# Seven stretches of an attention stage get written orders of TensorE, VectorE and ScalarE, and the softmax's join stands in one piece

## The chip, the cores and the metric

The kernel runs on one core of one Trainium2 chip. Its engines work side by side, each through a queue of its own in order: TensorE (PE, with its weight loads shown as PEld), VectorE (DVE), ScalarE (ACT), GpSimd (POOL) and SyncE (SP, which issues nearly all transfers). The metric is the device time of one execution in microseconds; the kernel before took 1698.79 us (median of three runs, 1698.14 to 1699.94).

## The reference

A decoder trunk of two layers over 512 tokens of width 1024: attention and a gated convolutional FFN, then a Mamba-2 mixer and a second FFN, all in float32. The change lies in the attention, cut here to what matters:

```python
def dilated_attention_mixer(h, w_qkv, w_o, cos, sin):
    qkv = (h @ w_qkv).reshape(bsz, s, N_ATTN_GROUPS, 3, HEADS, HEAD_DIM)   # 3 groups, 8 heads of 128
    q = apply_partial_rope(qkv[:, :, :, 0], cos, sin)                      # first 32 of 128 rotated
    k = apply_partial_rope(qkv[:, :, :, 1], cos, sin)
    for g in range(N_ATTN_GROUPS):                                         # dilations 1, 4, 16
        o_g, lse_g = dilated_window_attention(q[:, :, g], k[:, :, g], v[:, :, g], dil, steps)
    wts = jax.nn.softmax(jnp.stack(lses, axis=2), axis=2)
    o = jnp.einsum("bsgh,bsghe->bshe", wts, jnp.stack(outs, axis=2))
    return o.reshape(bsz, s, OUT_WIDTH) @ w_o
```

## The kernel before

The input stands transposed, in eight tiles of 128 features by 512 tokens, each as a high and a low part (`xh`, `xl`). Every product with weights is done in three passes: high x high, high x low, low x high. So each unit of weights (512 KB) comes by a transfer into one of four `raw` buffers, ScalarE casts its high part, and VectorE subtracts to get the low part (`load_unit`, L128). A unit is 24 products of TensorE over 512 tokens.

The opening computes the values of groups 1 and 2 for heads 0 to 3 (`first`, `second`, from `v_steps`), the sums of squares for the norm (`ssum`, then `ss` on TensorE, `ms` on VectorE, `rcol` on GpSimd), and `combine`: 32 small pieces on VectorE that form sums and differences of input tiles. These serve the pairs: for the query and key of one group, `qk_pair` uses seven half-width products in place of eight, from four weight pieces `a` to `d` (`load_sevens`: sums at L317 to L321, lows at L331).

Then one head after the other. `attend(h)` is a generator: the scores of four blocks of 128 queries (`scores`), maxima and exponentials, `join`, `by_key`, `values`. A row's two softmax parts (group 0; groups 1 and 2) lie on different partitions, so `join` copies 16 small pieces (`oth`, L591), then takes eight steps on 128x8 elements with one exponential between (L594 to L602). Its result, the share, multiplies the probabilities (`pr`, L609), which TensorE transposes (`pp`, L612) to multiply them with the values. Between these pieces TensorE computes the query, key and value of head h + 1 (`qk_step`, `qk_pair`, `v0_step`); VectorE reads each product, shuffles 32 rows (`rotqk`), and GpSimd turns them with two instructions of its own (L464 and L465, or L474 and L475).

What sets the order: TensorE's instructions stand as written wherever `tc.manual_schedule` names PE. VectorE's and ScalarE's are placed by the framework's scheduler, which sets each instruction of those engines where it reckons its operands ready.

Of the kernel before, what the change touches and what calls it, by code (L numbers as in the profile page):

```python
# [53 lines left out]
def trunk(ctx: ExitStack, tc: tile.TileContext, A, out):  # L54
# [12 lines left out]
    s3 = att.__enter__()  # L67
# [363 lines left out]
    dma(mask, A["mask"])  # L431
    V.tensor_tensor(cr, cr, rbc, op=ALU.mult)
    V.tensor_tensor(sr[0:ROPE, :], sr[0:ROPE, :], rbc[0:ROPE, :], op=ALU.mult)
# [20 lines left out]

    def qk_step(h, g, c, cut=None):
        n = f"qk{h}{g}{c}"
        p = project(A["wqk"][h * 7 + 2 * g + c], n, cut=cut)
        t = t2(n, "qk", 10, s3)
        at, of = (in_blocks, by_residue) if g == 0 else ((lambda ap: ap),) * 2
        V.tensor_tensor(at(t), of(p), of(cr), op=ALU.mult)  # L460
        rot = t2("rot" + n, "rot", 2, s3)
        R = slice(0, ROPE)
        V.stream_shuffle(rot[R, :], p[R, :], SWAP)  # L463
        G.tensor_tensor(rot[R, :], rot[R, :], sr[R, :], op=ALU.mult)  # L464
        G.tensor_tensor(at(t)[R], at(t)[R], of(rot)[R], op=ALU.add)  # L465
        qk[h, g, c] = t

    def turn(t, n):

        rot = t2("rot" + n, "rot", 2, s3)  # L470
        R = slice(0, ROPE)
        V.stream_shuffle(rot[R, :], t[R, :], SWAP)
        V.tensor_tensor(t, t, cr, op=ALU.mult)
        G.tensor_tensor(rot[R, :], rot[R, :], sr[R, :], op=ALU.mult)  # L474
        G.tensor_tensor(t[R, :], t[R, :], rot[R, :], op=ALU.add)  # L475

    def qk_pair(h, g):

        n = f"qk{h}{g}"
        sums, split_weights = load_sevens(  # L480
            A["wqs"][QK_PAIRS.index((h, g))], n, lambda n: t2(n, "sq", 2)
        )
        sums()
        w = {}
        r1, r3, r2 = (mm_bank(f"{n}r{i}")[:, 0:256] for i in (1, 3, 2))
        r4 = aux_bank(f"{n}r4")[:, 0:256]
        kept = t2("kept" + n, "ssum", 2)
        s1, s5 = kept[:, H0], kept[:, H1]
        q, k = (t2(f"{n}{c}", "qk", 10, s3) for c in range(2))

        def products(dst, t, at, operand, begin):
            if t not in w:
                w[t] = split_weights(t)
            for j in range(KD // 2):
                mm3(dst, *w[t], at + j, *operand(j), begin and j == 0, j == KD // 2 - 1, skip=True)

        def plain(b, h):
            return lambda j: (xh[2 * j + b][:, h], xl[2 * j + b][:, h])

        def other(i, h):  # L500
            return lambda j: [t[:, h] for t in combined[j][i]]

        products(r1, "a", 0, plain(0, H0), True)
        SC.copy(s1, r1)
        products(r3, "a", 4, other(0, H0), True)
        SC.copy(s5, r3)
        products(r2, "b", 0, other(0, H1), True)
        V.tensor_tensor(q[:, H1], s1, r2, op=ALU.add)
        products(r4, "b", 4, other(1, H1), True)
        products(r1, "c", 0, plain(1, H0), False)  # L510
        SC.copy(q[:, H0], r1)
        products(r3, "c", 4, plain(1, H1), False)
        V.tensor_tensor(q[:, H1], q[:, H1], r3, op=ALU.add)
        turn(q, n + "0")
        products(r2, "d", 0, other(1, H0), False)
        V.tensor_tensor(k[:, H0], s1, r2, op=ALU.add)
        V.tensor_tensor(k[:, H1], k[:, H0], s5, op=ALU.add)
        V.tensor_tensor(k[:, H0], k[:, H0], r4, op=ALU.add)
        turn(k, n + "1")
        qk[h, g, 0], qk[h, g, 1] = q, k  # L520

# [15 lines left out]
    def qk_steps(h):  # L537
        steps = []
        for g in range(NG):
            if (h, g) in QK_PAIRS:  # L540
                steps += [lambda g=g: qk_pair(h, g), lambda: None]
            else:
                steps += [lambda cut=None, g=g, c=c: qk_step(h, g, c, cut) for c in range(2)]
        return steps + [lambda: v0_step(h)]

# [3 lines left out]
    def attend(h):  # L549
# [35 lines left out]

        def join():

            V.tensor_copy(own[:, 2], own[:, 0])
            for a in range(4):
                for b in range(4):  # L590
                    V.tensor_copy(oth[32 * b : 32 * b + 32, :, :, a], own[32 * a : 32 * a + 32, 1:3, :, b])  # L591
            w = sm.tile([P, 5, 2, 4], F32, tag="join", name="join", bufs=2)
            top, ex, f = w[:, 0], w[:, 1:3], w[:, 3]
# [10 lines left out]

        def by_key(i):
            k0 = P if i == 0 else 0
            pr = prs[i]
            for w, cs in enumerate((slice(k0, 256), slice(256, 512))):
                V.tensor_scalar(pr[:, cs], pr[:, cs], share[:, w, i : i + 1], None, op0=ALU.mult)  # L609
            pp = (side_bank if i == 3 else aux_bank)("pp")  # L610
            for b in range(k0 // P, 4):
# [20 lines left out]
        scores(2)  # L632
        yield
        share = join()
        yield
        by_key(0)
        by_key(1)
        yield
        po, pg = aux_bank(f"po{h}"), aux_bank(f"pg{h}")
# [55 lines left out]

    with tc.manual_schedule(engines={mybir.EngineType.PE}):
        for f in qk_steps(0):
            f()

    def attend_and_project(h):  # L700

        core, fill = attend(h), qk_steps(h + 1)
        with tc.manual_schedule(engines={mybir.EngineType.PE}):
            next(core)
            v0_turn(h)
            fill[0]()
            fill[1]()
            next(core)
            next(core)
            for f in fill[2:5]:  # L710
                f()
            fill[5](cut=(2, lambda: next(core)))
            next(core)
            fill[6]()
            next(core, None)

    for h in range(NH):
        if h < NH - 2:
            attend_and_project(h)
            if h == STORED - 1:  # L720
                fetch_heads()
            if h == 3:
                for f in v_steps(1, 1)[1] + v_steps(2, 1)[1]:
                    f()
            continue
# [896 lines left out]
```

## Time and profile before

| what | us |
|---|---|
| median of three runs | 1698.79 |
| the profiled execution | 1699.21 |
| its span, first to last instruction | 1697.4 |
| the six heads 0 to 5, from the first product of head 0's stretch to that of head 6 | 382.76 |
| TensorE busy in the whole span | 1625.3 |
| VectorE busy in the whole span | 1235.5 |

A row of waits names the waiting engine, tile and line, then who released it, then the total in us, how many times, and the longest. A row of a stretch gives start and end, its length, the busy time of PE, PEld, DVE, ACT and POOL with the number of instructions, the clock granted to TensorE as a share of full speed, the share of the transfer engines, and GB/s. A row of a group gives line, engine, operation, output and inputs, count, busy us and mean ns of one, and the idle time ahead of it.

### The profile page before, as it was taken

To read this page: it belongs to the slowest core of one execution; us is meant where nothing else is said; L and a number is where in the kernel's file an instruction comes from. 1 tells how busy PE (TensorE), PEld (TensorE's weight loads), DVE (VectorE), ACT (ScalarE), POOL (GpSimd) and SP (SyncE) were. 2 spreads that over 40 slices of the span, in tenths; PEclk is the share of its full clock that TensorE was granted. 3 is DMA by queue.
4 is the path that set the end of the run, shared out by engine and by line. 5 is a ranking of instruction groups with operands and counts; after the bars stand their busy time and mean duration, and the time that the engine had idled before them with its cause. 6 is when DMAs were issued, how large, how long until landed. Compare 5 with 4: busy or idle time off the path is not lost.

```text
span 1697.4 us, 23559 instructions
## 1 busy us (share of the span) xinstructions
PE 1625.3 (96%) x8902; PEld 1416.5 (83%) x8902; DVE 1235.5 (73%) x2094; ACT 727.5 (43%) x1137; POOL 578.7 (34%) x432
## 2 busy tenths in 40 slices
PE   8987798997989999999999999999999999999998
PEld 6876687786878888998998888888888888988987
DVE  8566765637666677886875789989789777876874
ACT  6322232332423454444444545544444445344343
POOL 0253433304234245455333123212222356365230
PEclk8998898998989999999999999999999999999999
DMA  6222121321322332342332343332233232342241
GB/s 225 79 81 75 63 69 63 106 81 56 99 89 75 124 112 70 99 143 75 100 119 96 114 143 119 112 122 96 88 109 134 75 106 69 100 143 69 88 136 51
DMA packets 61889, 168.45 MB, mean 99 GB/s; under 512 B 7184, under 2 KB 10640, under 8 KB 61776
## 3 DMA queue, kind: packets, MB, share of 16 engines
q1 hardware_dynamic: 61216, 166.42, 29.5%
q8 instruction: 70, 1.15, 0.3%
q10 hardware_dynamic: 560, 0.53, 0.1%
q14 instruction: 43, 0.35, 0.1%
HBM read 163.19 MB, written 3.74 MB: 98 GB/s over the span
## 4 chain that ended last, share of the span: by engine, by line
PE 87%; DVE 9%; issue 2%; DMA 1%; ACT 1%; POOL 0%; SPq 0%; DVEq 0%; POOLq 0%; ACTq 0%
PE u L136 28%; PE qk L136 8%; PE v L136 6%; PE xs L136 5%; PE wso L136 5%; PE z L136 5%; PE b L136 3%; PE c L136 3%; PE wo L136 3%; PE wd L136 2%; PE wz L136 2%; DVE pr L609 1%; PE pp L612 1%; PE py L1195 1%; DVE oth L591 1%
## 5 line engine op out<-in xcount | busy, mean ns | idle before, releaser
L136 PE MATMUL u<-xh,hi_u 128*128 128x512 f32 x704 | 270.2, 384 | 0.0
L136 PE MATMUL u<-xh,lo_u 128*128 128x512 f32 x704 | 269.6, 383 | 0.0
L136 PE MATMUL u<-xl,hi_u 128*128 128x512 f32 x704 | 267.7, 380 | 0.0
L136 PEld LDWEIGHTS u<-xh,lo_u 128*128 128x128 f32 x704 | 131.9, 187 | 24.6
L128 DVE TENSOR_TENSOR lo_u<-raw_u,hi_u 128x1024 fp32r<-128x1024 f32 x88 | 124.3, 1422 | 38.6 <-ACT hi_u L127 38.5
L136 PEld LDWEIGHTS u<-xl,hi_u 128*128 128x128 f32 x704 | 132.0, 187 | 24.1
L136 PEld LDWEIGHTS u<-xh,hi_u 128*128 128x128 f32 x704 | 131.9, 187 | 22.5 <-issue 0.4
L127 ACT CAST hi_u<-raw_u 128x1024 fp32r<-128x1024 f32 x88 | 91.7, 1046 | 107.0 <-PE u L136 62.5
L464 POOL TENSOR_TENSOR rotqk<-rotqk,sr 32x512 f32<-32x512 f32 x32 | 54.2, 1694 | 224.5 <-DVE rotqk L463 214.1
L764 DVE SCALAR_TENSOR_TENSOR au<-u,par,au 128x511 f32<-128x511 f32 (+1 forms) x152 | 113.4, 746 | 20.4 <-ACT au L762 18.0
L789 POOL TENSOR_TENSOR au<-au,au 128x512 f32<-128x512 f32 x43 | 58.1, 1350 | 170.7 <-DVE au L764 156.9
L136 PE MATMUL qk<-xh,hi_qk 128*128 128x512 f32 x256 | 105.0, 410 | 0.1
L136 PE MATMUL qk<-xh,lo_qk 128*128 128x512 f32 x256 | 102.0, 398 | 0.0
L136 PE MATMUL qk<-xl,hi_qk 128*128 128x512 f32 x256 | 101.8, 398 | 0.0
L777 DVE TENSOR_TENSOR u<-u,rbc 128x512 f32<-128x512 f32 x76 | 52.9, 696 | 65.9 <-PE u L136 65.6
L1140 POOL TENSOR_TENSOR xdd<-xdt,dec 128x384 f32<-128x384 f32 x16 | 18.0, 1139 | 241.0 <-DVE xdt L1139 241.0
L460 DVE TENSOR_TENSOR qk<-qk,cr 128x512 f32<-128x512 f32 x32 | 22.0, 687 | 83.3 <-PE qk L136 83.2
L612 PE MATMUL pp<-ident,pr 128*128 128x128 f32 x120 | 24.0, 334 | 50.3 <-DVE pr L609 50.3
L762 ACT ACTIVATE au<-u,par 128x512 f32<-128x512 f32 x76 | 59.1, 778 | 23.0 <-DVE u L777 21.4
L612 PEld LDWEIGHTS pp<-ident,pr 128*128 128x128 f32 x120 | 16.0, 165 | 57.5 <-DVE pr L609 55.8
L239 POOL TENSOR_TENSOR ssum<-ssum,sq 128x512 f32<-128x512 f32 x21 | 32.5, 1549 | 84.4 <-ACT sq L238 84.0
L940 POOL TENSOR_TENSOR xr<-xr,sums 128x512 f32<-128x512 f32 x16 | 33.1, 2068 | 82.1 <-DVE sums L938 82.1
(3428 smaller groups left out, 4957.8 us busy)
## 6 DMA issues: line engine op xcount, KB each, us to landing
raw_u<-in_wup SPq DMA_DIRECT2D x88, 512.0 KB, 3.3
raw_qk<-in_wqk SPq DMA_DIRECT2D x32, 512.0 KB, 3.2
raw_xs<-in_win SPq DMA_DIRECT2D x16, 512.0 KB, 3.3
raw_z<-in_win SPq DMA_DIRECT2D x16, 512.0 KB, 3.3
lm<-rows SPq DMA_DIRECT2D x32, 256.0 KB, 5.0
raw_wso<-in_wso SPq DMA_DIRECT2D x16, 512.0 KB, 3.3
raw_v<-in_wv SPq DMA_DIRECT2D x12, 512.0 KB, 3.3
raw_wd<-in_wdn SPq DMA_DIRECT2D x16, 384.0 KB, 3.1
```

The source lines that it names most:

```text
L127: SC.copy(hi[:, s], raw[:, s])
L128: low.tensor_tensor(lo[:, s], raw[:, s], hi.bitcast(F32)[:, s], op=ALU.subtract)
L136: T.matmul(in_turns(dst), w, in_turns(x), start=first, stop=last, skip_group_check=skip)
L239: add.tensor_tensor(ssum, ssum, sq, op=ALU.add)
L460: V.tensor_tensor(at(t), of(p), of(cr), op=ALU.mult)
L464: G.tensor_tensor(rot[R, :], rot[R, :], sr[R, :], op=ALU.mult)
L612: T.transpose(pp[:, b * P : (b + 1) * P], pr[:, b * P : (b + 1) * P], ident)
L762: latest["tap"] = SC.activation(dst, src, AF.Identity, bias=col(c_b), scale=col(c_w + taps - 1))
L764: V.scalar_tensor_tensor(dst[:, j:], src[:, : S - j], col(c_w + taps - 1 - j), dst[:, j:], op0=ALU.mult, op1=ALU.add,)
L777: V.tensor_tensor(dst, p, rbc, op=ALU.mult)
L789: by.tensor_tensor(ab[1], ab[0], ab[1], op=ALU.mult)
L940: G.tensor_tensor(low3, low3, v.unsqueeze(1).to_broadcast([P, 2, 256]), op=ALU.add)
```

## The change

Seven stretches (from the second value product to the end of head 0's queries and keys, and the stretch of each of the heads 0 to 5) now stand in `manual_schedule` blocks for PE, DVE and Activation, so that these three engines take their instructions as written. For that, `qk_step` is cut into product and read, the loads into steps of their own (`ready`), `qk_pair` into the class `Pair` (sums, splits, seven blocks, the query's and the key's sums, swap and turn), and `by_key` loses the multiplication (`weigh`) and `join` the copies (`spread`). In a head, TensorE's first transposes move nine products later. In the first head's part, the plain product of the key moves behind both pairs. `combine` runs in the written stretch. The late values of head 3 are loaded two units ahead. One warm-up product (two instructions) is gone. Heads 6 and 7 keep the old order by `together`.

```diff
+            combine(0)
...
-    for j in range(KD // 2):
-        combine(j)
-    with tc.manual_schedule(engines={mybir.EngineType.PE}):
-        for f in second:
-            f()
-        T.matmul(warm[:, 0:P], ones, ones, start=True, stop=True)
...
+    def ready(h, g, c):
+        u = A["wqk"][h * 7 + 2 * g + c]
+        loaded[name_of(h, g, c)] = load_unit(u, name_of(h, g, c))
...
+    class Pair:
...
+        def key(self):
+            k = self.out[1]
+            V.tensor_tensor(k[:, H0], self.s[0], self.r[2], op=ALU.add)
+            V.tensor_tensor(k[:, H1], k[:, H0], self.s[1], op=ALU.add)
+            V.tensor_tensor(k[:, H0], k[:, H0], self.r[3], op=ALU.add)
+            self.swap(1)
+            self.turn(1)
+
+        def swap(self, c):
+            R = slice(0, ROPE)
+            rot = self.rot[c] = t2(f"rot{self.n}{c}", "rot", 2, s3)
+            V.stream_shuffle(rot[R, :], self.out[c][R, :], SWAP)
+            G.tensor_tensor(rot[R, :], rot[R, :], sr[R, :], op=ALU.mult)
+
+        def turn(self, c):
+            R = slice(0, ROPE)
+            t = self.out[c]
+            V.tensor_tensor(t, t, cr, op=ALU.mult)
+            G.tensor_tensor(t[R, :], t[R, :], self.rot[c][R, :], op=ALU.add)
+            qk[self.h, self.g, c] = t
...
+    WRITTEN = {E.PE, E.DVE, E.Activation}
+
+    with tc.manual_schedule(engines=WRITTEN):
+        load2(1)
+        V.tensor_tensor(cr, cr, rbc, op=ALU.mult)
+        second[0]()
+        combine(1)
+        load2(2)
...
+        second[3]()
+        one.sums()
+        one.split("ab")
+        p = qk_products(0, 0, 0)
+        qk_read(0, 0, 0, p)
+        one.split("cd")
...
+        two.key()
+        ready_v0(0)
+        p = qk_products(0, 0, 1)
+        qk_read(0, 0, 1, p)
+        ready(1, 0, 0)
+        v0_step(0)
+        ready(1, 0, 1)
...
     def attend_and_project(h, after=()):
+        core, m = attend(h), h + 1
+        follow = lambda c: ready(m + 1, 0, c)
+        with tc.manual_schedule(engines=WRITTEN):
+            pair = Pair(m, 1)
             next(core)
+            pair.sums((0,))
             v0_turn(h)
+            pair.split("a")
+            pair.sums((1,))
+            p = qk_products(m, 0, 0)
+            qk_read(m, 0, 0, p)
+            pair.split("bc")
+            ready(m, 2, 0)
+            p = qk_products(m, 0, 1)
+            qk_read(m, 0, 1, p)
+            next(core)
+            for i in range(3):
+                pair.block(i)
+            pair.query(0)
+            pair.split("d")
+            ready(m, 2, 1)
+            for i in range(3, 5):
+                pair.block(i)
+            next(core)
+            pair.block(5)
+            pair.query(1)
             next(core)
             next(core)
+            pair.block(6)
+            pair.turn(0)
+            pair.key()
+            ready_v0(m)
+            p = qk_products(m, 2, 0)
+            qk_read(m, 2, 0, p)
+
+            def cut():
+                next(core)
+                next(core)
+
+            p = qk_products(m, 2, 1, cut=(5, cut))
+            next(core)
+            qk_read(m, 2, 1, p)
+            for f in after[:2] or (lambda: follow(0), lambda: follow(1)):
+                f()
+            v0_step(m)
             next(core, None)
```

In the generator, each `next(core)` now runs to the next of nine stops: scores of blocks 0 and 1; of 2 and 3; `spread`; `join`; `weigh(0)` and `weigh(1)`; `by_key(0)` and `by_key(1)`; `weigh(2)` and `weigh(3)`; `values(0)`, `by_key(2)`, `by_key(3)`, `values(1)`; the rest.

Three places where the instructions move. First VectorE in head 1, around the join (`oth` and `join` its tiles, `qk21` head 2's pair, `lo_` and `raw` weights); before:

```order
L591 COPY oth<-own 32x4 x16
L128 TENSOR_TENSOR lo_qk_1734<-raw_qk_1732,hi_qk_1733 128x1024
L594 TENSOR_TENSOR join<-own,oth 128x8
L128 TENSOR_TENSOR lo_v_1815<-raw_v_1813,hi_v_1814 128x1024
L595 TENSOR_TENSOR join<-own,join 128x8
L596 TENSOR_TENSOR join<-oth,join 128x8
...
L600 TENSOR_TENSOR join<-join 128x8
L517 TENSOR_TENSOR qk_1576<-qk_1576,keptqk_1574 128x256
L318 TENSOR_TENSOR rawb_qk_2013<-rawa_qk_2012 128x512
L321 TENSOR_TENSOR q_qk_2015<-rawa_qk_2012,q_qk_2015 128x512
L601 RECIPROCAL join<-join 128x8
```

and now:

```order
L670 COPY oth<-own 32x4 x16
L527 TENSOR_TENSOR qk_1562<-qk_1562,qk21r_1558 128x256
L541 STREAM_SHUFFLE rotqk_1668<-qk_1562 32x512
L676 TENSOR_TENSOR join<-own,oth 128x8
L677 TENSOR_TENSOR join<-own,join 128x8
L678 TENSOR_TENSOR join<-oth,join 128x8
L680 TENSOR_TENSOR join<-own,join 128x8
L681 TENSOR_TENSOR join<-oth,join 128x8
L682 TENSOR_TENSOR join<-join 128x8
L683 RECIPROCAL join<-join 128x8
L684 TENSOR_TENSOR join<-join 128x8
L691 TENSOR_SCALAR pr<-pr,join 128x128
```

The eight steps of the join follow each other; the work for later weights has left this place. Second, the same engine and head a little later, at the other four multiplications; only now:

```order
L691 TENSOR_SCALAR pr<-pr,join 128x256 x3
L547 TENSOR_TENSOR qk_1562<-qk_1562,cr 128x512
L532 TENSOR_TENSOR qk_1563<-keptqk_1561,qk21r_1559 128x256
L533 TENSOR_TENSOR qk_1563<-qk_1563,keptqk_1561 128x256
L534 TENSOR_TENSOR qk_1563<-qk_1563,qk21r_1560 128x256
L541 STREAM_SHUFFLE rotqk_1702<-qk_1563 32x512
L547 TENSOR_TENSOR qk_1563<-qk_1563,cr 128x512
L128 TENSOR_TENSOR lo_v_1709<-raw_v_1707,hi_v_1708 128x1024
L465 TENSOR_TENSOR qk_1738<-qk_1713,cr 128x512
L468 STREAM_SHUFFLE rotqk_1740<-qk_1713 32x512
L691 TENSOR_SCALAR pr<-pr,join 128x256 x4
```

Before, all eight multiplications followed each other in one run (L609, x8 in the profile); now four stand ahead of the query's and key's turns and four behind, and the latter also behind the read of a product. Third, VectorE in the opening, between two sums of squares (`ssum`); before:

```order
L239 TENSOR_TENSOR ssum<-ssum,sq 128x512
L407 SCALAR_TENSOR_TENSOR ta3l<-d_419,par,ta3h 128x256
L415 TENSOR_TENSOR tb1l<-d_381,tb1h 128x256
L412 SCALAR_TENSOR_TENSOR d_400<-xp_218,par,t_401 128x256
L415 TENSOR_TENSOR tb3l<-t_420,tb3h 128x256
L415 TENSOR_TENSOR ta3l<-t_420,ta3h 128x256
L239 TENSOR_TENSOR ssum<-ssum,sq 128x512
```

and now:

```order
L239 TENSOR_TENSOR ssum<-ssum,sq 128x512
L228 SCALAR_TENSOR_TENSOR xl_98<-xp_259,par,xh_89 128x512
L128 TENSOR_TENSOR lo_v_252<-raw_v_250,hi_v_251 128x512
L239 TENSOR_TENSOR ssum<-ssum,sq 128x512 x2
L265 TENSOR_SCALAR ms<-ss 128x4
L128 TENSOR_TENSOR lo_v_316<-raw_v_314,hi_v_315 128x1024
L404 TENSOR_TENSOR d_325<-xp_119 128x256
```

The pieces of `combine` (L404 to L415) have left the opening and stand behind `ms`.

More of the change, by code (lines that the diff above doesn't have):

```diff
@@ L466, in qk_step @@
         qk[h, g, c] = t
[L468 to L493, printed above, removed]
-            for j in range(KD // 2):
[L495 to L520, printed above, removed]
@@ L537, in qk_steps @@
     def qk_steps(h):
[L538 to L544, printed above, removed]
+        return [
+            lambda cut=None, g=g, c=c: qk_step(h, g, c, cut) for g in range(NG) for c in range(2)
+        ] + [lambda: v0_step(h)]
+    E = mybir.EngineType
+    WRITTEN = {E.PE, E.DVE, E.Activation}
[5 more added lines that the diff above has]
+        load2(2)
+        V.tensor_tensor(sr[0:ROPE, :], sr[0:ROPE, :], rbc[0:ROPE, :], op=ALU.mult)
+        second[1]()
+        combine(2)
+        load2(3)
+        second[2]()
+        combine(3)
+        ready(0, 0, 0)
+        one = Pair(0, 1)
+        second[3]()
[4 more added lines that the diff above has]
+        one.split("cd")
+        two = Pair(0, 2)
+        for i in range(3):
+            one.block(i)
+        one.query(0)
+        two.sums()
+        two.split("a")
+        for i in range(3, 6):
+            one.block(i)
+        one.query(1)
+        two.split("b")
+        one.block(6)
+        one.turn(0)
+        one.key()
+        two.split("cd")
+        for i in range(3):
+            two.block(i)
+        two.query(0)
+        ready(0, 0, 1)
+        for i in range(3, 6):
+            two.block(i)
+        two.query(1)
+        two.block(6)
+        two.turn(0)
+        two.key()
[5 more added lines that the diff above has]
+        ready(1, 0, 1)
     scale = HD ** -0.5
@@ L584, in scores, with spread @@
                     )
-        def join():
+        def spread():
             V.tensor_copy(own[:, 2], own[:, 0])
@@ L694, in wo_first, with together, attend_and_project @@
         wo_held[m] = (hi, lo, p)
[L696 to L703, printed above, removed]
+    def together(core):
+        for n in (1, 1, 2, 2, 2, 1):
+            for _ in range(n):
+                next(core, None)
+            yield
+    def attend_and_project(h, after=()):
+        core, m = attend(h), h + 1
+        follow = lambda c: ready(m + 1, 0, c)
+        with tc.manual_schedule(engines=WRITTEN):
+            pair = Pair(m, 1)
@@ L715, in attend_and_project @@
+            qk_read(m, 2, 0, p)
[6 more added lines that the diff above has]
+            for f in after[:2] or (lambda: follow(0), lambda: follow(1)):
+                f()
+            v0_step(m)
             next(core, None)
+            for f in after[2:]:
+                f()
+            if after:
+                follow(0)
+                follow(1)
@@ L717, in trunk, with late_values @@
+    def late_values():
+        (l1, s1), (l2, s2) = v_steps(1, 1), v_steps(2, 1)
+        loads = [lambda l=l, u=u: l(u) for l in (l1, l2) for u in range(4)]
+        steps = s1 + s2
+        out = loads[:2]
+        for i, f in enumerate(steps):
+            if i + 2 < len(loads):
+                out.append(loads[i + 2])
+            out.append(f)
+        return out
     for h in range(NH):
         if h < NH - 2:
-            attend_and_project(h)
+            attend_and_project(h, late_values() if h == 3 else ())
```

85 lines of the change are left out of this document (69 added, 16 removed).

## The prediction

> **What bounds the kernel now.** I read the page first: which engine is nearly always busy, and where it is not.
>
> ```profile
> PE 1625.3 (96%) x8902; PEld 1416.5 (83%) x8902; DVE 1235.5 (73%) x2094; ACT 727.5 (43%) x1137; POOL 578.7 (34%) x432
> PE   8987798997989999999999999999999999999998
> PEclk8998898998989999999999999999999999999999
> ```
>
> TensorE (PE) is the bound, and what it lacks, some 72 of 1697.4 us, lies in the first 13 slices (42 us each), the attention; there its clock dips too. So a gain must come from PE's waits there. Next, PE's waits up to 600 us:
>
> ```profile
> PE pp L612 <- DVE pr L609: 50.3, 18, 7.8
> PE sc L571 <- POOL qk L475: 7.2, 1, 7.2
> PE v L136 <- DVE lo_v L128: 2.9, 2, 2.0
> PE ss L260 <- DVE ssum L239: 2.6, 1, 2.6
> ```
>
> 50.3 us is one wait, repeated: the transposes of the probabilities (`pp`) wait until VectorE has multiplied them by the softmax's share. The other rows are single waits before the first head. Third, one stretch per head, from its first projection product to the next head's (columns: length, then busy time of PE, PEld, DVE, ACT, POOL, granted clock, DMA share):
>
> ```profile
> 109.06:166.90 57.84, 48.70 (x279) 42.74 (x278) 35.55 (x82) 16.68 (x31) 22.30 (x12) 0.91 0.18 57
> 166.90:224.78 57.88, 48.73 (x278) 42.80 (x278) 37.13 (x92) 17.67 (x35) 22.28 (x12) 0.88 0.20 69
> 224.78:282.70 57.92, 48.77 (x279) 42.85 (x278) 37.15 (x92) 17.66 (x35) 22.28 (x12) 0.88 0.21 69
> 282.70:377.15 94.45, 90.88 (x470) 78.54 (x470) 47.45 (x104) 31.43 (x51) 21.17 (x12) 0.96 0.26 88
> 377.15:434.16 57.01, 47.84 (x279) 42.12 (x278) 36.85 (x88) 17.66 (x35) 22.32 (x12) 0.91 0.19 62
> 434.16:491.82 57.66, 48.21 (x278) 42.34 (x278) 37.84 (x93) 20.47 (x40) 18.37 (x12) 0.91 0.27 93
> ```
>
> Five heads lose about 9.1 us each; head 3, which also computes late values, loses 3.57 (94.45 - 90.88). Head 1 cut in four shows the price:
>
> ```profile
> 166.90:195.60 28.70, 28.70 (x174) 25.69 (x173) 19.70 (x62) 11.63 (x28) 9.37 (x6) 1.00 0.24 79
> 195.60:206.75 11.15, 2.00 (x8) 1.24 (x8) 11.15 (x22) 1.22 (x2) 8.22 (x4) 0.60 0.27 94
> 206.75:211.17 4.42, 4.42 (x13) 3.46 (x12) 1.09 (x3) 0.58 (x1) 1.26 (x1) 0.50 0.00 0
> 211.17:224.78 13.61, 13.61 (x88) 12.42 (x87) 5.19 (x7) 4.25 (x5) 3.42 (x2) 0.99 0.15 49
> ```
>
> PE waits 9.15 us (11.15 - 2.00) while VectorE is busy throughout; then it works 4.42 us at clock 0.50, 2.21 too many; the seven transposes in the hole, also at the low clock, lose some 1.0. So a head without the hole takes 57.88 - 9.15 - 2.21 - 1.0 = **45.5 us**. VectorE's 37.13 us would fit, 8 to spare: it is late by its order, not by its amount.
>
> **The heads.** The products stay. VectorE's order is now written: the spreading copies, the eight small steps of the join, then four multiplications, with no next-head work between, where before eight large instructions stood between the join's first and last step. PE gets 9 more products ahead of the first transposes (39 instead of 30). Durations, head 1:
>
> ```profile
> L609 DVE TENSOR_SCALAR pr<-pr,join x64: 257/335/1409, 144.5 to 554.8; 128x256 f32<-128x256 f32 x56, 128x128 f32<-128x128 f32 x8
> L128 DVE TENSOR_TENSOR lo_qk<-raw_qk,hi_qk 128x1024 fp32r<-128x1024 f32 x4 | 5.5, 1370 | 0.0
> L609 DVE TENSOR_SCALAR pr<-pr,join 128x256 f32<-128x256 f32 (+1 forms) x8 | 4.9, 676 | 0.0
> L463 DVE STREAM_SHUFFLE rotqk<-qk 32x512 f32<-32x512 f32 x4 | 2.9, 723 | 0.0
> L460 DVE TENSOR_TENSOR qk<-qk,cr 128x512 f32<-128x512 f32 x4 | 2.7, 687 | 12.4 <-PE qk L136 12.4
> L591 DVE COPY oth<-own 32x4 f32<-32x4 f32 x16 | 2.6, 163 | 0.2
> L598 DVE TENSOR_TENSOR join<-own,join 128x8 f32<-128x8 f32 x1 | 1.2, 1234 | 0.0
> L331 DVE TENSOR_TENSOR loa_qk<-rawa_qk,hia_qk 128x1024 fp32r<-128x1024 f32 x1 | 1.2, 1212 | 0.0
> L508 DVE TENSOR_TENSOR qk<-keptqk,qk21r 128x256 f32<-128x256 f32 x1 | 0.4, 415 | 0.0
> L594 DVE TENSOR_TENSOR join<-own,oth 128x8 f32<-128x8 f32 x1 | 0.2, 159 | 0.0
> ```
>
> Now the clock runs from the third block of the pair's products, whose end lets VectorE go on. It comes 16.5 us after the head's first product (48 long products at 0.222 us, two scores 1.7, 36 short ones at 0.117: all inside the 28.70 us row). From there VectorE does, in its written order: first query sum 0.42, two lows 1.9 (one half as wide), spreading 2.8, second query sum 0.42, shuffle 0.72, eight small steps at 0.16 with some 0.5 for ScalarE's exponential, 1.8, four multiplications at 0.335, 1.3: **9.4 us**. PE comes to the first transposes at 28.70 + 9 x 0.222 = 30.7, that is 14.2 us after the block. Covered by 4.8 us; if PE's nine extra products were not there, by 2.8.
>
> The second four multiplications are the tight place. Before them stand the query's turn 0.69, the key's three sums, shuffle and turn 2.7, the low of the value weights 1.2, the read of the first late product 1.4; with their own 1.3 VectorE needs 9.4 + 7.3 = 16.7, less 1.4 for about twenty overlaps of 0.07 between rows. PE arrives 17.4 us after the block (seven transposes, nine products, three short ones later), at the last four transposes 0.5 later. Undisturbed, VectorE is 2 us early. But in head 1 the multiplications took 676 ns on average instead of the median 335 (2.7 us more in eight), and L598 took 1234 ns where its like take 159 (1.1 more), both beside working POOL, and POOL's rotations now stand beside this place. With these 3.8 us VectorE is 1.7 us late. Bounds: 0 (nothing disturbs), and 4.3 us if five neighbouring POOL instructions cost VectorE their full 1.27 (the row is in part (d)). I take **1.7 us** a head, the value of the measured delays, plus 0.5 of low clock: 47.7 us. Then 288.31 (five heads) - 5 x 47.7 = 49.8; head 3 gets 3.57 + 2.0 of clock - 2.2 = 3.5 back. **Together 53.3 us.** Queued behind a late multiplication are the read of the last late product and two lows, 3.8 us, and then the scaling of the values; that waits for the values' product (24 x 0.222 = 5.3 us) anyway, so the multiplications are all that PE feels.
>
> **The first head.** Two terms. The 32 pieces of the combined operands leave the opening for the time behind the norm:
>
> ```profile
> 3.70:32.40 28.70, 23.18 (x94) 18.26 (x92) 27.74 (x60) 22.93 (x44) 0.00 (x0) 0.91 0.69 241
> 27.00:28.80 1.80, 1.80 (x7) 1.34 (x5) 1.80 (x5) 0.88 (x3) 0.00 (x0) 0.52 0.75 280
> 32.00:37.30 5.30, 5.27 (x16) 4.52 (x17) 3.68 (x5) 1.17 (x2) 1.85 (x1) 0.50 0.49 151
> 4.91:18.60 13.69, 13.68 (x58) 11.02 (x57) 12.82 (x27) 12.61 (x27) 0.00 (x0) 1.00 1.03 371
> 38.56:96.60 58.04, 58.04 (x343) 51.31 (x341) 36.94 (x52) 20.67 (x28) 19.57 (x8) 1.00 0.30 98
> 96.60:108.71 12.11, 3.63 (x15) 3.12 (x15) 7.88 (x17) 2.02 (x5) 8.03 (x5) 0.73 0.30 109
> 222.63:224.54 1.91, 1.91 (x19) 1.86 (x17) 1.14 (x2) 1.08 (x1) 0.00 (x0) 1.00 0.16 28
> L412 DVE SCALAR_TENSOR_TENSOR d<-xp,par,t 128x256 f32<-128x256 f32 x4 | 1.9, 487 | 0.0
> L404 DVE TENSOR_TENSOR d<-xp 128x256 f32<-128x256 f32 x4 | 1.7, 421 | 0.0
> 25.83 0.49 PE L136 MATMUL v<-lo_v,xh 128*128 128x512 f32 x1 [1.97 <-DVE lo_v L128]
> ```
>
> VectorE is full there (27.74 of 28.70). Without 32 pieces of 0.42 to 0.49 (14.4 us, 11.8 with overlaps), the sums of squares are ready by 18 to 21 us instead of 32, and PE becomes what `ss` waits for. At 18.60 PE, which had run without a wait since 4.91, has 28 of the 84 products in front of `ss` left; at 0.23 each they end at 25.0, where they now end at 29.2 with 2.9 us of waits and 1.80 us at clock 0.52. So `ss` starts at 25.0 instead of 32.0, and the 5.30 us at clock 0.50 behind it, worth 2.6, may go as well: 9.7 at most. I take **8.7**, since VectorE and ScalarE still follow the loads (DMA share 1.03). The pieces then fill VectorE while PE does 96 products; VectorE had 36.94 of those 58.04 us busy, so 11.8 more fit, but 48.7 of 58.04 leaves little at each step, and the low of the first query weights stands behind all 32 pieces; I charge **1.0**. Second, between 96.60 and 108.71 PE does 1.9 us worth of scores and transposes (the row from 222.63 has the same work at full clock) and waits for POOL's rotation of the key; the written order puts one plain product (the first group's key) and the values' product behind the second pair, 10.6 us of PE, of which the values' 5.3 cover the last rotation (two POOL instructions). Up to 10.2; I take **8.7**. Bounds for the three: 8 (either term missing) and 19.9; sum **16.4**.
>
> The loads move with the steps: SP issues the same transfers one after the other, still through four buffers, each freed by a low, at a DMA share of 0.18 to 0.27; I cost them at nothing. What hides them is that each unit's products take 5.3 us; without that cover a late load shows as PE waiting for a low behind a DMA. Two dropped warm-up products are 0.1 us. Heads 6 and 7 stay with the scheduler.
>
> Sum: 16.4 + 53.3 = 69.7 from this execution's 1699.21 us (span 1697.4 and 1.8 around it): 1629.5. The runs' median lies 0.4 lower: **1629 us**.
>
> **The clock and a rule.** After the 1.97 us wait at 25.83 the clock fell to 0.52 from 27.00 to 28.80: a wait of 2 us can cost clock here. The Trainium skill ("TensorE: Matmul & The Clock Gate", Why this matters for your kernels) asks only that no idle gap exceed about 3 us. By that rule the remaining 1.7 us would cost no clock, 3 us less in six heads, 1626; the row above speaks against it.
>
> **Rivals.** (a) No wait remains anywhere: heads at 45.5 and the first head at its bound, 5 x 12.16 + 5.6 + 19.9 = 86.3, 1612 us. For it: VectorE's spare 8 us a head; against it: POOL's delays.
> (b) The wait returns at the second multiplications at its upper bound, 4.3 us with 2.2 of low clock: 52.0 a head, 28.3 + 0 + 16.4 = 45, 1654 us.
> (c) The opening's gain is lost again because the 32 pieces hold up the value weights: 53.3 + 4 (half of the second term), 1641 us. For it: the full VectorE in the 3.70 row; against it: VectorE now idles some 5 us in front of `ms`, and before had spare time in the same 58 us.
> (d) Slower: POOL starves.
>
> ```profile
> 87.66 8.11 POOL L474 TENSOR_TENSOR rotqk<-rotqk,sr 32x512 f32<-32x512 f32 x1 [1.71 <-DVE rotqk L472]
> 194.69 5.31 POOL L475 TENSOR_TENSOR qk<-qk,rotqk 32x512 f32<-32x512 f32 x1 [1.20 <-DVE qk L473]
> L464 POOL TENSOR_TENSOR rotqk<-rotqk,sr x32: 1270/1630/2248, 67.9 to 533.1; 32x512 f32<-32x512 f32 x32
> ```
>
> Such an instruction takes 1.27 us alone and took 5.31 and 8.11 beside a packed VectorE, which is what the change makes. Each head has twelve. At 5.3 us each POOL needs 63.6, and the next head's scores wait for it: 5 x 5.9 (63.6 less 57.7) slower, head 3 the same, less 16.4: 1712 us. It decides from a mean of 5.1, where a head costs 61 us and the first head's gain is eaten up; now it is 22.28/12 = 1.9, and shuffles, reads from PSUM and small steps keep letting POOL in. The Trainium skill says the same ("GPSIMD Engine Reference", Specifications: it shares its SBUF interfaces with VectorE and contends where VectorE reads two SBUF inputs); these rows agree.
> (e) The orders bind nothing: 1699. The rows in the order part speak against it.
>
> **How the numbers follow.** Forecast 0.47; (a) 0.20, (b) 0.13, (c) 0.13, (d) 0.05, (e) 0.02. The range 1611 to 1657 takes in (a) to (c). Faster by over 0.2% (3.4 us; less can't be told from no change): 0.93; within: 0.02; slower: 0.05.
>
> **What would show it.** Right: `pp` waits under 15 us in total, heads of 46 to 49 us, `ss` at 25 us, the first head's products at 89 to 93, VectorE's share up, POOL's instructions longer. Wrong: PE waiting for POOL's `qk` at the scores (d), for lows in the second value product (c), `pp` waits of 4 us a head (b), or a clock row under 0.95 in every head.

## The result, and the profile after

The changed kernel takes **1653.62 us** (median of four runs, 1652.85 to 1654.64), the kernel before 1698.73 us beside it: a ratio of 0.9734, 95% interval 0.9717 to 0.9751, 45 us less. The forecast was 1629 us with a range of 1611 to 1657; the time lies in the range, near its upper end, and within 1 us of rival (b). One execution of experiment 9, which took 1823 us at a mean granted clock of 0.849, is left out of that experiment's median.

The page of the changed kernel, engine totals and two rows of the 40 slices:

```profile
PE 1616.7 (98%) x8900; PEld 1410.5 (85%) x8900; DVE 1258.4 (76%) x2094; ACT 723.8 (44%) x1137; POOL 567.7 (34%) x432
...
PE   9999999999899999999999999999999999999998
...
PEclk9999999999999999999999999999999999999999
```

The notches of the first 13 slices are nearly gone, and no slice shows a low clock any more. TensorE still idles 34 us (1651.1 - 1616.7). TensorE's waits up to 560 us:

```profile
PE pp L698 <- DVE pr L691: 19.7, 20, 1.7
PE qk02r L136 <- DVE loc_qk L331: 2.3, 1, 2.3
PE po L706 <- ACT pt L700: 2.1, 1, 2.1
PE qk02r L136 <- DVE qk L532: 1.1, 1, 1.1
```

The transposes (`pp`) still wait for the multiplications (`pr`): 19.7 us in place of 50.3, twenty times, none over 1.7 us. One row per head, 0 to 5 (columns as before: length, busy time of PE, PEld, DVE, ACT, POOL, clock, DMA share):

```profile
93.23:143.66 50.43, 47.33 (x281) 42.16 (x279) 40.13 (x92) 17.23 (x35) 20.71 (x12) 0.97 0.27 84
143.66:194.50 50.84, 47.49 (x280) 42.03 (x278) 40.68 (x92) 17.23 (x35) 20.71 (x12) 0.97 0.24 78
194.50:245.32 50.82, 47.41 (x280) 41.97 (x279) 40.73 (x92) 17.25 (x35) 20.71 (x12) 0.97 0.24 78
245.32:340.12 94.80, 91.23 (x472) 78.77 (x470) 49.53 (x108) 30.36 (x55) 20.74 (x12) 0.96 0.25 81
340.12:392.38 52.26, 48.66 (x278) 42.84 (x278) 41.48 (x84) 17.25 (x32) 20.75 (x12) 0.93 0.25 81
392.38:445.30 52.92, 48.70 (x283) 42.77 (x281) 44.83 (x98) 22.11 (x43) 20.98 (x12) 0.94 0.33 110
```

The first head's product stands at 93.23 us, before at 108.71: 15.5 us. The six heads take 352.07 us instead of 382.76: 30.7 us, all of it in the five ordinary heads; head 3 gains nothing (94.80 against 94.45). Together 46.2 of the 46.3 us by which the spans differ. Head 1 cut in four shows where an ordinary head still loses:

```profile
143.66:177.90 34.24, 34.24 (x208) 30.74 (x205) 29.66 (x78) 13.09 (x30) 13.33 (x8) 1.00 0.25 85
177.90:184.22 6.32, 2.97 (x19) 2.27 (x18) 5.92 (x11) 1.71 (x3) 4.29 (x4) 0.91 0.18 44
184.22:186.75 2.53, 2.53 (x8) 2.02 (x8) 2.10 (x2) 1.35 (x2) 2.45 (x2) 0.54 0.01 3
186.75:194.50 7.75, 7.75 (x51) 7.00 (x50) 3.00 (x3) 1.08 (x1) 0.64 (x1) 1.00 0.33 101
```

Up to 177.90 there is no wait: the first transposes are covered. At the second four multiplications TensorE idles 3.35 us (6.32 - 2.97), and then it works at clock 0.54. VectorE is busy for 5.92 of these 6.32 us and GpSimd (POOL) for 4.29. The opening:

```profile
3.70:32.40 28.70, 28.70 (x135) 24.35 (x134) 21.90 (x39) 19.10 (x34) 1.85 (x1) 1.00 0.82 284
60.00:91.33 31.33, 27.15 (x173) 24.73 (x172) 26.51 (x35) 8.68 (x12) 18.14 (x11) 0.95 0.31 95
91.33:93.23 1.90, 1.90 (x17) 1.84 (x16) 1.70 (x2) 0.00 (x0) 0.00 (x0) 1.00 0.00 0
```

```profile
24.24 0.28 PE L260 MATMUL ss<-ones,ssum 128*128 128x1 f32 x2
```

From 3.70 to 32.40 us TensorE never waits and the clock is full; `ss` starts at 24.24 instead of 32.03. The first scores and transposes take 1.90 us, where before 12.11 us passed. What is new is the row from 60.00: 4.2 us of waits (31.33 - 27.15) in the second pair of head 0 and the products behind it.

### The profile page after: what moved, and what is told of

Same layout as the page of the kernel before. It is cut to its first block, busy times and chain, and to the rows that moved or that the text cites. A ratio compares the mean times of both kernels' runs of the same rounds, so it can differ in the third digit from the quotient of the medians.

```text
span 1651.1 us, 23543 instructions
## 1 busy us (share of the span) xinstructions
PE 1616.7 (98%) x8900; PEld 1410.5 (85%) x8900; DVE 1258.4 (76%) x2094; ACT 723.8 (44%) x1137; POOL 567.7 (34%) x432
## 4 chain that ended last, share of the span: by engine, by line
PE 71%; DVE 3%; issue 1%; ACT 0%; POOL 0%; POOLq 0%; DVEq 0%; ACTq 0%
PE u L136 28%; PE xs L136 5%; PE wso L136 5%; PE z L136 5%; PE b L136 3%; PE c L136 3%; PE wo L136 3%; PE wd L136 2%; PE wz L136 2%; PE qk L136 1%; PE py L1338 1%; PE pf L1346 1%; PE pst L1293 1%; PE v L136 1%; PE wd113r L136 1%
## 5 line engine op out<-in xcount | busy, mean ns | idle before, releaser
L469 POOL TENSOR_TENSOR rotqk<-rotqk,sr 32x512 f32<-32x512 f32 x32 | 64.7, 2023 | 206.2 <-DVE rotqk L468 206.2
L920 DVE TENSOR_TENSOR u<-u,rbc 128x512 f32<-128x512 f32 x76 | 52.9, 696 | 66.0 <-PE u L136 65.7
L136 PE MATMUL qk<-xh,hi_qk 128*128 128x512 f32 x256 | 99.4, 388 | 0.4 <-ACT hi_qk L127 0.4
L136 PE MATMUL qk<-xh,lo_qk 128*128 128x512 f32 x256 | 98.3, 384 | 0.5 <-DVE lo_qk L128 0.5
L136 PE MATMUL qk<-xl,hi_qk 128*128 128x512 f32 x256 | 97.3, 380 | 0.0
L660 ACT ACTIVATE pr<-pr,neg 128x256 f32<-128x256 f32 (+1 forms) x64 | 31.1, 487 | 68.2 <-DVE neg L658 67.6
L136 PEld LDWEIGHTS qk<-xh,lo_qk 128*128 128x128 f32 x256 | 47.9, 187 | 9.9 <-DVE lo_qk L128 1.0
L1392 POOL TENSOR_TENSOR lm<-lm,cb 128x512 f32<-128x512 f32 x32 | 47.4, 1506 | 25.5 <-ACT lm L1325 25.5
```

The costliest lines, as they stand in the source:

```text
L136: T.matmul(in_turns(dst), w, in_turns(x), start=first, stop=last, skip_group_check=skip)
L660: SC.activation(pr[:, cs], pr[:, cs], AF.Exp, bias=neg[:, w, i : i + 1], scale=scale, accum_out=own[:, w, 1, i : i + 1],)
L920: V.tensor_tensor(dst, p, rbc, op=ALU.mult)
L1392: G.tensor_tensor(t, t, cb, op=ALU.mult)
```

## The experiments

The question after the result was why the transposes still wait. **Theory A**: GpSimd's turns, beside which the second four multiplications now stand, stretch VectorE's instructions, by more than the prediction took. **Theory B**: VectorE simply has too much to do up to this place.

**1. The second four multiplications behind the first four.**

```diff
         weigh(0)
         weigh(1)
+        weigh(2)
+        weigh(3)
         yield
...
-        weigh(2)
-        weigh(3)
         yield
```

> VectorE's second four multiplications stand directly behind the first four in every head; all else as in the change. Theory A (VectorE is late at this place because GpSimd's turns, which run beside it, stretch its instructions with two inputs; the work between the two groups of multiplications is what comes too late): the multiplications are done some 5 us before TensorE wants them, the 19.7 us of pp waits and about 2 us of low clock a head go, heads 45.5 to 47 us, total 1621 to 1628. Theory B (VectorE has too much to do up to this place, wherever the multiplications stand): the wait moves to the value weights' low or to the read of the late key product, heads stay over 49.5 us, total 1648 to 1656.

Measured: 1622.2 us, ratio 0.955 (0.9536 to 0.9564). Heads 0 and 1, head 3, head 5:

```profile
93.84:139.01 45.17, 45.17 (x280) 40.82 (x279) 37.94 (x92) 17.14 (x35) 21.60 (x12) 1.00 0.30 94
139.01:184.49 45.48, 45.40 (x281) 40.82 (x279) 38.47 (x92) 17.11 (x35) 21.61 (x12) 1.00 0.27 88
...
229.72:318.06 88.34, 87.94 (x472) 76.68 (x470) 47.15 (x108) 30.26 (x55) 21.62 (x12) 1.00 0.27 87
...
364.36:414.06 49.70, 45.58 (x280) 40.73 (x279) 43.01 (x102) 23.04 (x43) 25.40 (x12) 1.00 0.39 127
```

TensorE has next to no wait in heads 0 to 2 and the clock is full; head 3 gains 6.5 us. The place in VectorE's order is what cost the time: 31 us for moving four instructions a head. In heads 0 to 4 nothing behind them became late, although GpSimd's busy time did not fall (21.6 us a head). This favours A over B, as B expected the wait to move on; but it does not yet show what makes the place late.

**2. The same order without GpSimd.**

```diff
+            if 1 <= self.h <= 6:
+                return
             G.tensor_tensor(rot[R, :], rot[R, :], sr[R, :], op=ALU.mult)
```

(and the same at the other turns; the queries and keys of heads 1 to 6 stay unrotated).

> GpSimd's two turns of each query and key (32 of 128 rows rotated) are left out for heads 1 to 6, so these heads' queries and keys are not rotated; VectorE's order stays. Theory A (GpSimd's turns stretch VectorE's instructions with two inputs): low of the value weights back from 2.30 to about 1.3 us, third key sum from 1.36 to 0.42, multiplications from 1.25 to 0.335 each; VectorE is early, pp waits under 3 us in total, heads 45.5 to 46.5, total 1620 to 1628. Theory B (VectorE's written work alone is too long): the same waits, total 1648 to 1656.

Measured: 1615.3 us, ratio 0.9509 (0.9493 to 0.9525), with VectorE's order untouched. VectorE's groups in head 1, first in the change, then without the turns (line, operation, output and inputs, count, busy us, mean ns, idle ahead):

```profile
L691 DVE TENSOR_SCALAR pr<-pr,join 128x256 f32<-128x256 f32 x7 | 4.1, 644 | 0.0
...
L128 DVE TENSOR_TENSOR lo_v<-raw_v,hi_v 128x1024 fp32r<-128x1024 f32 x1 | 2.3, 2303 | 0.0
...
L533 DVE TENSOR_TENSOR qk<-qk,keptqk 128x256 f32<-128x256 f32 x1 | 1.4, 1365 | 0.0
L678 DVE TENSOR_TENSOR join<-oth,join 128x8 f32<-128x8 f32 x1 | 1.3, 1254 | 0.0
```

```profile
L695 DVE TENSOR_SCALAR pr<-pr,join 128x256 f32<-128x256 f32 x7 | 2.0, 338 | 0.0
...
L128 DVE TENSOR_TENSOR lo_v<-raw_v,hi_v 128x1024 fp32r<-128x1024 f32 x1 | 1.2, 1222 | 0.0
...
L534 DVE TENSOR_TENSOR qk<-qk,keptqk 128x256 f32<-128x256 f32 x1 | 0.4, 424 | 0.0
...
L682 DVE TENSOR_TENSOR join<-oth,join 128x8 f32<-128x8 f32 x1 | 0.2, 162 | 0.0
```

And head 1 as a stretch, without the turns:

```profile
137.19:182.33 45.14, 45.14 (x281) 40.74 (x279) 33.22 (x92) 17.03 (x35) 0.00 (x0) 1.00 0.28 88
```

Its second four multiplications and the transposes that need them:

```profile
168.97 1.11 DVE L695 TENSOR_SCALAR pr<-pr,join 128x256 f32<-128x256 f32 x4
171.50 1.04 PE L702 MATMUL pp<-ident,pr 128*128 128x128 f32 x8
```

This settles it for A. Between the spreading copies and the last multiplication GpSimd costs VectorE 7 x 0.306 = 2.1 us at the multiplications, 1.08 at the low of the value weights, 0.94 at a key sum, 1.09 at one step of the join: 5.3 us. Undisturbed, the four are done at 170.08, which is 1.4 us before TensorE begins the transposes and some 2 us before it comes to the last of them. TensorE's 3.35 us of idle time in the change are what is left of the 5.3 after this margin; with the low clock behind them gone too, the head takes 45.14 us. What GpSimd does and does not stretch is to be seen in the change's head 1, VectorE's rows first, then GpSimd's:

```profile
175.85 2.30 DVE L128 TENSOR_TENSOR lo_v<-raw_v,hi_v 128x1024 fp32r<-128x1024 f32 x1
178.08 0.68 DVE L465 TENSOR_TENSOR qk<-qk,cr 128x512 f32<-128x512 f32 x1
175.29 1.78 POOL L542 TENSOR_TENSOR rotqk<-rotqk,sr 32x512 f32<-32x512 f32 x1 [1.68 <-DVE rotqk L541]
177.14 2.13 POOL L548 TENSOR_TENSOR qk<-qk,rotqk 32x512 f32<-32x512 f32 x1
```

`lo_v` stands beside two turns and takes 2.30 us; the product's read at L465 begins inside the second turn and takes 0.68 us, its usual time. It reads one operand from PSUM. The turns themselves take 1.78 and 2.13 us instead of 1.27.

**3. The turns on VectorE.** `G.tensor_tensor` becomes `V.tensor_tensor` at the four turns.

> The turns are done by VectorE in place of GpSimd, in the same places of the order (0.69 us each by the like row of 32 rows and more). Theory A: up to the second four multiplications VectorE gets about six turns, 4.1 us, and loses about 4.8 us of stretching: the heads stay as they are within 1.5 us, total 1646 to 1662. Theory B: 4.1 us more wait in each of six heads and more in the opening, total 1675 to 1690.

Measured: 1657.9 us, ratio 0.9764 (0.9748 to 0.978). Head 1 as a stretch, then the wait:

```profile
143.34:194.97 51.63, 47.07 (x281) 42.39 (x279) 41.45 (x104) 17.14 (x35) 0.00 (x0) 0.97 0.24 77
```

```profile
PE pp L698 <- DVE pr L691: 26.0, 7, 7.1
```

VectorE does six turns of 0.68 us more up to this place, 4.1 us, and a head is 0.8 us longer than with GpSimd. So GpSimd's help with these six turns is worth about 1 us; it takes back nearly all that it spares.

**4. More turns on GpSimd.** Two instructions without use behind the key's first turn:

```diff
             G.tensor_tensor(rot[R, :], rot[R, :], sr[R, :], op=ALU.mult)
+            if c == 1 and 1 <= self.h <= 6:
+                G.tensor_tensor(rot[R, :], rot[R, :], sr[R, :], op=ALU.add)
+                G.tensor_tensor(rot[R, :], rot[R, :], sr[R, :], op=ALU.subtract)
```

> Two more GpSimd instructions of 32x512 in each of heads 1 to 6, behind the key's first turn (sr is added and subtracted again); VectorE's order and work stay. Theory A (GpSimd's running instructions stretch VectorE's): all of the second four multiplications and the read ahead of them fall beside a busy GpSimd, 1 to 2 us more wait a head, total 1660 to 1668. If GpSimd's amount does not matter and the stretch is a fixed cost, or VectorE's own work is the limit: 1651 to 1656.

Measured: 1656.7 us, ratio 0.975 (0.9731 to 0.9768): between the two expectations, and not told apart from the change. The rows go A's way: the multiplications take 781 ns on average instead of 644, TensorE stops four times in place of three, 0.8 us each (head 1). Since most of the place was beside a busy GpSimd already, two more instructions could add little; the run decides nothing by its time.

**5. TensorE's order alone.**

```diff
-    WRITTEN = {E.PE, E.DVE, E.Activation}
+    WRITTEN = {E.PE}
```

> The same program text as the change, but only TensorE's order is binding; VectorE's and ScalarE's instructions go where the scheduler puts them. If VectorE's order is what removed the waits: pp waits back at 35 to 60 us, total 1685 to 1705. If it is TensorE's nine extra products and the earlier loads: total 1650 to 1665.

Measured: **1647.7 us**, ratio 0.9696 (0.9681 to 0.971): faster than the change, by 6 us. Neither expectation allowed for that. Its waits, then VectorE's multiplications in head 1:

```profile
PE pp L698 <- DVE pr L691: 10.3, 6, 2.8
PE sc L650 <- POOL qk L470: 9.5, 4, 2.5
PE sc L648 <- POOL qk L470: 8.7, 1, 8.7
```

```profile
182.30 2.11 DVE L691 TENSOR_SCALAR pr<-pr,join 128x128 f32<-128x128 f32 x8
```

The scheduler again spreads the join, over 9 us (171.71 to 180.83) and with nine other instructions between its steps, and yet `pp` waits only 1.6 us in most heads: it sets all eight multiplications side by side (2.11 us, beside an idle GpSimd). It pays elsewhere, as the scores wait for GpSimd again. In all, TensorE idles 35.9 us (1644.8 - 1608.9), about as much as the change's 34.4; the 6 us lie in the clock (0.993 against 0.989), at which the same 8900 instructions are busy 1608.9 us instead of 1616.7. So the join in one piece is not what removed the wait, and the binding orders of VectorE and ScalarE as written here remove hardly more waiting than the scheduler does, for the place of four instructions; with these moved (experiment 1) they are worth 25 us.

**6. The kernel before with one number changed.**

```diff
-            fill[5](cut=(2, lambda: next(core)))
+            fill[5](cut=(5, lambda: next(core)))
```

> The kernel before with one number changed: in heads 0 to 5 TensorE does nine more late products (2.0 us) ahead of the first transposes; VectorE's order stays as it was, row by row. If TensorE's order alone made most of the gain that came with TensorE alone written (head 1 from 57.9 to 51.2): pp waits from 50.3 to under 20, total 1655 to 1668. If nine products only cover their own length: 2.0 us less wait in each of five heads and up to 1 us of clock, total 1683 to 1690. If the wait moves to the second transposes: 1694 to 1701.

Measured: 1682.9 us, ratio 0.991 (0.9893 to 0.9926).

```profile
PE pp L612 <- DVE pr L609: 38.8, 18, 5.7
```

```profile
164.11:219.37 55.26, 48.07 (x281) 42.26 (x279) 37.17 (x92) 17.67 (x35) 22.33 (x12) 0.91 0.23 72
```

Nine products cover about their own length, as the second expectation has it: 15 us, a third of the change's gain, by one digit and with VectorE's order as it was.

**7. The change with the nine products put back**: `cut=(2, cut)` in place of `cut=(5, cut)`.

> The change with the nine products put back behind the first transposes (VectorE's order as in the change but for two rows at the heads' ends). By the prediction's margin the first multiplications are still 2.8 us early: no wait at the first transposes, and the second ones come at the same time: 1651 to 1656. If the nine products are what covers the first multiplications: a wait there of 1 us or more in each head, 1658 to 1668.

Measured: 1649.9 us, ratio 0.9718 (0.9701 to 0.9736), not told apart from the change. There is no wait at the first transposes in any head from 0 to 5, `pp` waits 20.8 us in all, 19.4 of them at the second ones of these heads. With VectorE's order written the nine products aren't needed.

**8. The opening's pieces put back.** `combine` returns to its place ahead of the norm, the rest stays:

```diff
-            combine(0)
...
+    for j in range(KD // 2):
+        combine(j)
     with tc.manual_schedule(engines=WRITTEN):
         load2(1)
```

> Only the 32 pieces of the combined operands go back ahead of the norm, where the scheduler mixes them with the sums of squares; the rest as in the change. If the pieces are what delays ss: ss at 31 to 33 us instead of 24.2, the second value product 9 to 10.4 us later; of the 4.2 us of waits that TensorE now has in the second pair of head 0 some part goes, since VectorE has nothing to make up there. Total 1653.6 + 10 - 1 to 4 = 1660 to 1663. If the charge for making up is nothing (those waits come from GpSimd's turns alone), 1663 to 1664.5. If the pieces do not matter, 1653.

Measured: 1663.9 us, ratio 0.9788 (0.9771 to 0.9806).

```profile
31.12 1.87 PE L260 MATMUL ss<-ones,ssum 128*128 128x1 f32 x8 [3.69 <-DVE ssum L239]
```

```profile
PE qk02r L136 <- DVE loc_qk L331: 2.3, 1, 2.3
PE qk02r L136 <- DVE qk L531: 1.0, 1, 1.0
```

`ss` is at 31.12 us and the first head's product at 103.41 instead of 93.23: the pieces' place is worth 10.2 us. The waits in the second pair are the same 2.3 and 1.0 us with the pieces out of the way, so they aren't the pieces' price.

**9. The whole opening of before under the new heads**, in two runs; the rows are the second run's.

> The opening up to the end of head 0's queries and keys stands in the order of before (combined pieces in front of the norm, TensorE alone written, the first group's key ahead of the pairs); heads 0 to 5 as in the change. If the two parts add up: 1653.6 plus the 15.5 us that the first head came earlier, 1669 (1665 to 1673). If the heads lean on the opening's order (weights loaded ahead, VectorE free in time), slower: over 1676.

> The kernel with the opening of before and the heads of the change once more, for its rows. If the opening's parts are 10.2 us for the combined pieces, 5 us given back at the second pair of head 0, and little for GpSimd at the first scores, since the second pair's turns come ahead of the values here too: first head's product 6 to 7 us later than in the change, at 99 to 100.5 us, with ss at 31 to 33. If the wait for GpSimd is there in full: at 107 or later.

Measured: 1659.9 us (median of three executions, ratio 0.977, 0.9754 to 0.9786), and 1655.0 in the second run's single execution.

```profile
31.57 1.05 PE L260 MATMUL ss<-ones,ssum 128*128 128x1 f32 x8 [2.06 <-DVE ssum L239]
97.41 0.49 PE L633 MATMUL sc<-qk,qk 128*128 128x128 f32 x2 [1.78 <-POOL qk L547]
```

The first expectation (1669) was wrong. The first head's product comes at 98.97, 5.7 us later than in the change. It pays the 10.2 us for the pieces and 1.8 us of the wait for GpSimd, and has none of the change's 4.2 us of waits in the second pair and of the low clock behind them. (That execution ends only 2.1 us after the change's, as its six heads take 348.5 us instead of 352.1.) So the long wait for GpSimd at the first scores goes without the plain key product being moved behind the pairs. Experiment 5 is the counterpart: there the key product stands behind the pairs as in the change, VectorE's places are the scheduler's, and the first scores wait 8.7 us. In that run and in the kernel before, VectorE does sums and lows of head 1's pair among the second pair's turns; in the change and here it does not. I take this mixing for the reason. The two runs bear it out, but other instructions move with it, and no run changes it alone.

**10. Repairs on top of experiment 1.** In the opening the first pair's key sums and a low go ahead of two turns; heads 0 to 3 come back from memory at the end of head 5's stretch.

```diff
-        one.turn(0)
-        one.key()
-        two.split("cd")
+        one.key_sums()
+        two.split("c")
+        one.turn(0)
+        one.swap(1)
+        one.turn(1)
+        two.split("d")
...
+            if h == STORED - 1:
+                fetch_heads((0, 1))
             v0_step(m)
```

> Three edits on the change: the second four multiplications directly behind the first four (measured alone: 1622.2); in the opening the first pair's key sums and the low of the second pair's third weights ahead of the two turns; the return of heads 0 to 3 from memory at the end of head 5's stretch, so that ScalarE's copies of pt do not stand behind casts that wait for that transfer. From the waits of the run with the first edit: 2.3 + 1.1 in the opening, 2.4 + 1.8 in head 5, and one to three us of low clock behind them: 1613 to 1618. If the second and third only move the waits on: 1620 to 1624.

Measured: 1619.1 us, ratio 0.953 (0.9513 to 0.9547), the lowest of the versions that leave nothing out. First, from experiment 1, ScalarE's cast that its queue held, and TensorE's wait behind it; then head 5 and the waits now:

```profile
399.47 0.62 ACT L753 CAST o4h<-raw_o 128x512 fp32r<-128x512 f32 x1 [6.00 <-DMA raw_o<-store]
400.52 0.49 PE L706 MATMUL po<-pt,v 128*128 128x128 f32 x2 [2.36 <-ACT pt L700]
```

```profile
361.40:408.51 47.11, 46.94 (x285) 41.77 (x284) 42.53 (x97) 20.87 (x41) 21.97 (x12) 1.00 0.31 101
```

```profile
PE v L136 <- DVE lo_v L128: 2.1, 1, 2.1
```

The return of stored heads has no written order, so the scheduler had set its casts into head 5's stretch, where ScalarE waited 6.00 us for a transfer with the copies of `pt` queued behind. Head 5 falls from 49.70 to 47.11 us, and the first head's product comes at 90.93 instead of 93.84. The profiled spans differ by 4.5 us (1615.9 and 1620.4), but the ratios' intervals overlap: against experiment 1 the gain is likely, not certain.

**11. One repair more**: `ready_v0(0)` goes four blocks ahead, for the 2.1 us above.

> The kernel with the three edits, and a fourth: the load and split of head 0's value weights stand ahead of the second pair's last four blocks, where VectorE is idle 1.2 us. The wait of 2.1 us for lo_v and some low clock behind it go: 2 to 3 us under 1619, 1615 to 1618. If that low only pushes the key's turns back and the scores wait for GpSimd: 1618 to 1621.

Measured: 1621.1 us, ratio 0.9545 (0.9531 to 0.9559), no gain.

```profile
89.41 0.49 PE L654 MATMUL sc<-qk,qk 128*128 128x128 f32 x2 [3.03 <-POOL qk L470]
```

The wait for `lo_v` is gone, and the scores wait 3.03 us for GpSimd in its place, as the second expectation has it.

## Why the prediction came out as it did

**The bound and the direction** were right: TensorE's waits in the attention were the reserve, and all 46 us of the gain lie in front of 446 us.

**The first head**: 16.4 us forecast, 15.5 measured, but by terms that were off both ways. The early `ss` was put at 25.0 us and came at 24.24; the second value product starts 10.4 us earlier (28.16 against 38.56) where I took 8.7 and called 9.7 the most. VectorE and ScalarE were not the limit that I allowed for, and the clock stayed at 1.00. The wait at the first scores went in full, 10.2 us instead of 8.7, but hardly for the reason given: with the plain key product in its new place and VectorE's order free, 8.7 us of wait are there (experiment 5), and with the product in its old place 1.8 (experiment 9). That this term came out near its size is luck. The charge of 1.0 us for making up was mis-sized: from 28.16 to 91.33 us 63.17 us pass where before 58.04 did, 4.2 us of waits and some 0.9 of low clock. And its reason was wrong: experiment 8 has the same waits without the pieces. In their place the rows show VectorE's turns and sums ahead of the third low, `loc_qk`; experiment 10 takes that wait away by the order alone.

**The heads**: 47.7 us forecast, 50.4 to 52.9 measured. The first transposes are covered, as forecast. At the second multiplications VectorE was to be 2 us early undisturbed; experiment 2 shows 1.4 us at the first of these transposes and some 2 at the last. **The step that failed is the size of the disturbance**: 3.8 us, copied from two groups of the head before, where it is 5.3, because the value weights' low and a key sum now run beside turns too. I had the upper bound (4.3 us of wait) and chose low in it. The second term, 0.5 us of low clock, was worse: 50.84 - 45.14 - 3.35 = 2.35 us in head 1. So 1.65 us of wait and 1.85 us of clock more than forecast, less 0.36 since the floor is 45.14 and not 45.5: the 3.14 us by which head 1 is over 47.7. Heads 4 and 5 lose 1.4 and 2.1 us more than head 1; in head 5 stands the 2.1 us wait behind ScalarE, which no term had. Of the signs named ahead, `ss` and the first head's product came as called; `pp` (19.7 us, not under 15) and the heads (not 46 to 49 us) did not.

**Head 3** was to give 3.5 us and gave none: three waits for multiplications, 3.2 us, stand there as in the other heads. Without them (experiment 1) it gives 6.1. The sum itself, 3.57 + 2.0 - 2.2, is 3.4, and no row gives its 2.0 us of clock.

**The reason for the heads' gain** was wrong in part. I credited VectorE's written order and the join in one piece. Experiment 5 idles hardly longer (35.9 us against 34.4) without either, experiment 6 gets 15 us from TensorE's nine products alone. What the rest of the 51 us of experiment 5 comes from (loads as steps of their own, the cut of the generator, which the scheduler also follows) was not taken apart.

**The rivals.** (b) is what happened: 52.0 us a head and 1654 us by its terms, against 51.5 on average and 1653.6. That the totals agree to 1 us is partly luck: its wait of 4.3 us was 3.35 in head 1 (50.84 us), and heads 4 and 5 came to 52 us and more by other losses. I gave it 0.13, which the measured delays of 676 ns and 1234 ns should have raised. (d), a starving GpSimd, is far off: 20.71/12 = 1.7 us an instruction. (c) fell with experiment 8, (a) with the waits, (e) with the order's effect in experiments 1 and 5.

**The rule on the clock.** The prediction set a row (a 2 us wait that cost clock) against the Trainium skill ("TensorE: Matmul & The Clock Gate", Why this matters for your kernels), which asks for no idle gap over about 3 us. Here no wait of the heads exceeded 2.1 us, in heads 0 to 4 none exceeded 1.71 us, and the clock fell in every one of them. So keeping each gap under 3 us was not enough here; in head 1's row 3.35 us were idle out of 6.32.

## What to carry to other kernels

Where an order is written out for an engine, an instruction's place decides more than the order's binding: four multiplications of 0.34 us, set behind 7.8 us of other work (171.48 to 179.31 in head 1), cost 31 us over six heads. Put what the bound engine waits for ahead of everything that nobody waits for, and price instructions that will stand beside a second engine on the same memory by their stretched time. Before writing an order for three engines, try it for the bound one alone, and look for unordered code that the scheduler can still drop into it.

## What the runs showed of the hardware

A GpSimd instruction on 32x512 (1.27 us alone) held back a VectorE instruction that began beside it until GpSimd's was nearly over. In head 1 of the change the join's step of 128x8 that began at 168.03 us ended at 169.28, and GpSimd's ended at 169.26; the key sum from 172.53 ended at 173.89, GpSimd's at 173.61; the value weights' low from 175.85 ended at 178.15, the first of the two GpSimd instructions beside it at 177.07. So the price was about what was left of GpSimd's instruction, about 1 us in these three rows, whatever VectorE's size: 0.16 became 1.25 us, 0.42 became 1.37, 1.22 became 2.30. The second of these two, begun while the low still ran, took 2.13 us. The read from PSUM did not change (0.68). The Trainium skill ("GPSIMD Engine Reference", Specifications) names VectorE's instructions with two SBUF inputs, and those in a 2-port mode, as the ones that contend; the two-input rows agree. The multiplications, which have one tensor input, went from 338 to 644 ns on average, so either they run in such a mode or the list is short; no run tells which.

The clock could react to several short waits close together: in head 1 of the change, three of 1.62, 0.83 and 0.90 us within 6.32 us were followed by 2.53 us at 0.54. It did not always. In experiment 7 each of the six heads has such waits, 2.9 to 4.4 us in three pieces; behind them the clock was 0.50 in heads 1, 3 and 5 and 1.00 in heads 0, 2 and 4. Heads 1 and 2, behind waits of 1.22, 0.84, 0.89 us and of 1.22, 0.83, 0.90 us:

```profile
180.00:183.00 3.00, 3.00 (x13) 2.81 (x13) 1.75 (x4) 2.48 (x3) 2.07 (x2) 0.50 0.03 8
231.00:234.00 3.00, 3.00 (x17) 2.58 (x16) 1.98 (x3) 2.15 (x3) 2.63 (x2) 1.00 0.00 0
```

What decides between the two stays open. A difference of a few us between versions with the same waits, such as the 6 us of experiment 5, can come from it.
